# A third output-gate tile, one reset pattern for both scans, and a ScalarE table asked for by name, in a hybrid attention and recurrence block

## The chip, the cores and the metric

The kernel runs on one core of a Trainium2 chip. The metric is device microseconds for one execution; the time of a kernel is the median over its runs. Engines are named as in the profile: PE (TensorE matmul), PEld (its weight load), DVE (VectorE), ACT (ScalarE), POOL (GpSimd), SP (the queue that issues most transfers).

## The reference, cut to what matters

One encoder layer over 1024 tokens of width 1024. A shared RMSNorm and input projection feed a dilated windowed attention and a bidirectional gated recurrence; each branch is gated and projected, then the two are merged, projected and added to the input. The change is in the recurrence (8 heads of 128 channels, a forward scan and a backward scan):

```python
def gla_chunk_scan(q, k, v, log_f):
    b = jnp.cumsum(gc, axis=3)                 # of log_f, within a chunk
    q_t = qc * jnp.exp(b)
    k_t = kc * jnp.exp(-b)
    k_s = kc * jnp.exp(b_last[:, :, :, None, :] - b)
    a = jnp.where(lower, jnp.einsum('nbhik,nbhjk->nbhij', q_t, k_t), 0.0)
    o_intra = jnp.einsum('nbhij,nbhjv->nbhiv', a, vc)
    ...                                        # state = dec * state + k_s^T v;  o_inter = q_t state

def hgrn2_scan(q, i, z_f, lb):
    f = lb + (1.0 - lb) * jax.nn.sigmoid(z_f)
    return gla_chunk_scan(q, 1.0 - f, i, jnp.log(f))

o_fwd = hgrn2_scan(q_b, i_b, zf_fwd, lb_f)
o_bwd = ...                                    # the same on flipped inputs, with its own zf and lb
o_b = rms_norm(o_fwd + o_bwd, hg_norm_w[layer]) * jax.nn.silu(g_b)
```

So a head needs Sigmoid (forget gates, and the output gate of SiLU), Ln (of f, and inside the norm's inverse root), and Exp (of the sums, of the decays, and inside the norm's inverse root). [...]

## The kernel before, in words

The program is one long list of instructions for each engine, laid out by a planner in the source. `Plan` keeps a planned time for each engine and for each tile; every instruction goes through `Plan.note`, which adds an assumed duration and remembers which table ScalarE is assumed to hold (`table`: "sig", "exp" or "ln"; a switch is charged 1.28 us of planned ACT time). Work that isn't on the main line of projections is put down as tasks (`b.task`, for ACT, DVE, POOL or SP) or as products (`b.product`, for PE), each with the tiles that it needs; after every few projection matmuls the planner emits those whose inputs it takes to be ready. Each engine then runs its list in order, and waits at semaphores where data isn't there. So a changed planned duration or a free tile changes the order of everything behind it, on all engines.

The recurrence takes the span from about 950 to 1300 us. Per head h:

- four projections of 512 columns (`run_unit`, tiles gp) give the forget gates' inputs, evacuated by ACT into sk. Their fp32 operands are split into high and low parts; the weights' parts (whi, wlo) are made on ACT, with the rest added by a DMA of POOL.
- `logs(h)`: four Sigmoids over sk, `gates(h - 1)`, then four Ln into qr. Ahead of the Ln it asks by name for the table set that has both Ln and Exp. `gates` emits the Sigmoid of the output gate (gs from gb) of the previous head at once if its tile is there by the plan, or else leaves it as a task of its own.
- `sums`: a scan on DVE (Bc) that sums qr within chunks of 128, reset by a pattern of ones with a zero at each chunk's start (rst), then differences.
- `exps_b`: four Exp (km, km, qr, q); `decay_exp`: Exp of the decays G.
- `k_transpose` (PE, tile kT, from sk = km x G), a copy by ACT into an SBUF tile kT, `states` (PE, tile U, then the states S on DVE), `cross` (PE tiles X and Y, DVE into xa), `outputs` (PE tile oB, ACT squares it into on).
- `norm_out`, `norm_guess`, `scale_out`: DVE sums the squares (ssb); ACT does Ln, Exp and Square on 128x4 (oy, oz); DVE mends the factor; ACT scales oB into on. `out_transpose` (PE tile onT) then multiplies by the gate gb on DVE and stores.

The output gates' inputs lie in DRAM (gbD) and are loaded by SP into a ring of two tiles, gb, whose buffer comes free at `out_transpose`. Where a function's table isn't in, a load (ACT_TABLE_LOAD) stands in front of the instruction; where no set is asked for by name, the one for an Exp does not have Ln, and the one for an Ln does not have Exp.

Of the kernel before, what the change touches and what calls it, by code (L numbers as in the profile page):

```python
# [11 lines left out]
BF = mybir.dt.bfloat16  # L12
AF = mybir.ActivationFunctionType
OP = mybir.AluOpType
# [569 lines left out]
def hybrid_block(ctx, tc, a, out):  # L584
    b = Builder(ctx, tc, a)
    a_, v_, g_, t_, s_ = b.p.act, b.p.dve, b.p.pool, b.p.pe, b.p.sp
# [312 lines left out]
    for d in range(8):  # L899
        wh, wl = b.w[d]  # L900
        for j in range(4):
            c = slice(128 * j, 128 * j + 128)
# [666 lines left out]
    hp = bctx.enter_context(tc.tile_pool(name="hgrn", bufs=1))  # L1569
# [18 lines left out]
    a_.dma_start(mX, a["c_mx"])  # L1588
    a_.dma_start(mY, a["c_my"])
    BF = mybir.dt.bfloat16  # L1590
    rst = [hp.tile([128, 512], BF, name=f"rst{d}") for d in range(2)]
    for d in range(2):
        g_.memset(rst[d], 1.0)
        e = 0 if d == 0 else 127
        g_.memset(rst[d].rearrange("p (c t) -> p c t", c=4)[:, :, e:e + 1], 0.0)
    YB = hp.tile([128, 4, 64], F32, name="YB")
    g_.memset(YB, 0.0)

    ig_ring = b.ring(hp, "ig", 8, [128, 256])
    gb_ring = b.ring(hp, "gb", 2, [128, 512])  # L1600
    sk_ring = b.ring(hp, "sk", 7, [128, 512])
    qq_ring = b.ring(hp, "q", 2, [128, 512])
    qr_ring = b.ring(hp, "qr", 8, [128, 512])
# [50 lines left out]
    def c4(t):  # L1654
        return t.rearrange("p (c t) -> p c t", c=4)

    def start_head(h):
        st = dict(used={}, mm=[None, None], G=[None, None], QR={}, Q2={}, KM={}, S={}, s=0, qm=0, km=0)
        H[h] = st
        for d in range(2):  # L1660
            st["mm"][d] = mm_ring.get()
        b.task("act", [SK[h, d, u] for d, u in ORDER], lambda: logs(h), 4, lambda: qr_ring.soon(4))
# [6 lines left out]
    def gates(h):  # L1669
        for u in range(2):  # L1670
            here = lambda u=u: (h, u) in GB and b.when_all([GB[h, u]])
            if here():
                gate(h, u)
            else:
                b.task("act", [], lambda u=u: gate(h, u), 4, here)

    def logs(h):
        for d, u in ORDER:
            a_.activation(SK[h, d, u], SK[h, d, u], AF.Sigmoid)
        if h:  # L1680
            gates(h - 1)
        a_.preload_act_table_set("natural_log_exp_and_others")
        for d, u in ORDER:
            lf = qr_ring.get()
            a_.activation(lf, SK[h, d, u], AF.Ln, scale=omlb[:, d, h:h + 1], bias=lb[:, d, h:h + 1])
            b.task("dve", [lf], lambda d=d, u=u, lf=lf: sums(h, d, u, lf), 4, q2_ring.soon)

    def sums(h, d, u, lf):
        st = H[h]
        Bc = hp.tile([128, 512], F32, tag="Bc", name=b.name("Bc"), bufs=2)  # L1690
        if d == 0:
            v_.tensor_tensor_scan(Bc, rst[0], lf, 0.0, op0=OP.mult, op1=OP.add)
        else:
            v_.tensor_tensor_scan(Bc[:, ::-1], rst[1][:, ::-1], lf[:, ::-1], 0.0, op0=OP.mult, op1=OP.add)
        B4 = c4(Bc)
        at = slice(4 * u, 4 * u + 4)
        g_.tensor_copy(st["mm"][d][:, 0:2, at].rearrange("p k c -> p c k"), B4[:, :, 31 + d:97:64])
        g_.tensor_copy(st["mm"][d][:, 2, at], B4[:, :, LAST[d]])
        sec = slice(64, 128) if d == 0 else slice(0, 64)
        D1 = lf  # L1700
        v_.tensor_tensor(c4(D1), B4, B4[:, :, MID1[d]:MID1[d] + 1].to_broadcast([128, 4, 128]), op=OP.subtract)
        Q2 = q2_ring.get()
        v_.tensor_tensor(Q2, B4[:, :, sec], B4[:, :, MID2[d]:MID2[d] + 1].to_broadcast([128, 4, 64]),
                         op=OP.subtract)
        st["Q2"][d, u] = Q2
        b.task("act", [D1, Q2], lambda: exps_b(h, d, u, D1, Q2), 4, km_ring.soon)

    def exps_b(h, d, u, D1, Q2):
        st = H[h]
        fst, sec = (slice(0, 64), slice(64, 128)) if d == 0 else (slice(64, 128), slice(0, 64))  # L1710
        KM = km_ring.get()
        a_.activation(c4(KM)[:, :, fst], c4(D1)[:, :, fst], AF.Exp, scale=-1.0, bias=lomlb[:, d, h:h + 1])
        a_.activation(c4(KM)[:, :, sec], Q2, AF.Exp, scale=-1.0, bias=lomlb[:, d, h:h + 1])
        QR = D1
        a_.activation(QR, D1, AF.Exp)
        a_.activation(Q2, Q2, AF.Exp)
        st["QR"][d, u], st["KM"][d, u] = QR, KM
        b.task("dve", [KM], lambda: k_mul(h, d, u), 3)
        b.task("dve", [], lambda: q_mul(h, d, u), 5, lambda: (h, u) in QQ and b.when_all([QQ[h, u], QR, Q2]))
        if h == 7 and len(st["QR"]) == 4:  # L1720
            gates(h)
        if all((d, v) in st["QR"] for v in range(2)):
            b.task("dve", [st["mm"][d]], lambda: decay(h, d), 3, G_ring.soon)

    def decay(h, d):
        st = H[h]
        G = G_ring.get()
        mm = st["mm"][d]
        t = hp.tile([128, 8], F32, tag="Gt", name=b.name("Gt"), bufs=2)
        cur, nxt = (slice(0, 7), slice(1, 8)) if d == 0 else (slice(1, 8), slice(0, 7))  # L1730
        v_.tensor_tensor(t[:, cur], mm[:, 2, cur], mm[:, d, nxt], op=OP.add)
        v_.tensor_tensor(G[:, cur, d], t[:, cur], mm[:, d, cur], op=OP.subtract)
        v_.tensor_tensor(G[:, cur, 1 - d], t[:, cur], mm[:, 1 - d, cur], op=OP.subtract)
        b.task("act", [G], lambda: decay_exp(h, d, G, cur), 3)
        mm_ring.done(mm)

    def decay_exp(h, d, G, cur):
        a_.activation(G[:, cur, :], G[:, cur, :], AF.Exp)
        H[h]["G"][d] = G

    def k_mul(h, d, u):
        st = H[h]
        KM = st["KM"][d, u]
        v_.scalar_tensor_tensor(KM, SK[h, d, u], -1.0, KM, op0=OP.add, op1=OP.mult)
        st["km"] += 1
        b.task("dve", [KM], lambda: k_state(h, d, u), 3,
               lambda: st["G"][d] is not None and (h // 2, 4 * u + 3) in IG and b.when_all([st["G"][d]]))
        xready(h)
# [8 lines left out]
    def q_mul(h, d, u):  # L1757
        st = H[h]
        sec = slice(64, 128) if d == 0 else slice(0, 64)
        q = QQ[h, u]  # L1760
        v_.tensor_tensor(st["Q2"][d, u], st["Q2"][d, u], c4(q)[:, :, sec], op=OP.mult)
        v_.tensor_tensor(st["QR"][d, u], st["QR"][d, u], q, op=OP.mult)
        st["qm"] += 1
        if st["qm"] == 4:
            for v in range(2):
                qq_ring.done(QQ.pop((h, v)))
        xready(h)
# [125 lines left out]
    def norm_out(h, u, ps, on):  # L1893
        ss = tiny.tile([128, 4], F32, tag="ssb", name=b.name("ssb"), bufs=3)
        v_.tensor_reduce(ss, c4(on), axis=mybir.AxisListType.X, op=OP.add)
        b.task("act", [ss], lambda: norm_guess(h, u, ps, on, ss), 2)

    def norm_guess(h, u, ps, on, ss):
        y, y2 = (tiny.tile([128, 4], F32, tag=k, name=b.name(k), bufs=3) for k in ("oy", "oz"))
        a_.activation(y, ss, AF.Ln, scale=1.0 / 128, bias=eps)  # L1900
        a_.activation(y, y, AF.Exp, scale=-0.5)
        a_.activation(y2, y, AF.Square)

        def newton():
            v_.scalar_tensor_tensor(y2, ss, 128 * EPS, y2, op0=OP.add, op1=OP.mult)
            v_.scalar_tensor_tensor(y, y2, -384.0, y, op0=OP.add, op1=OP.mult)
            b.task("act", [y], lambda: scale_out(h, u, ps, on, y), 2)
        b.task("dve", [y2], newton, 2)

    def scale_out(h, u, ps, on, r):  # L1910
        for c in range(4):
            f0 = 128 * c
            a_.activation(on[:, f0:f0 + 128], ps[:, f0:f0 + 128], AF.Copy, scale=r[:, c:c + 1])
        b.bank.done(ps)
        b.product(7, [on], lambda: out_transpose(h, u, on),
                  lambda: stage.soon() and (h, u) in GI and b.when_all([GB[h, u]]), merge=False)
# [453 lines left out]
def _build(arrays):  # L2370
    import concourse.bacc as _bacc
    nc = _bacc.Bacc("TRN2", target_bir_lowering=False, num_devices=1)
    args = {n: nc.dram_tensor(f"in_{n}_dram", v.shape, mybir.dt.from_np(v.dtype), kind="ExternalInput").ap()
            for n, v in arrays.items()}
    out = nc.dram_tensor("out_0_dram", (S, D), F32, kind="ExternalOutput").ap()
    with tile.TileContext(nc) as tc:
        hybrid_block(tc, args, out)
    return nc
# [9 lines left out]
```

## Time and profile before

| what | value |
| --- | --- |
| median of 3 runs | 1510.41 us (1509.92 to 1513.04) |
| the profiled execution | 1511.62 us, its span 1509.8 us |
| PE busy, 950 to 1300 us | 329.21 of 350 us |
| ACT busy, 950 to 1300 us | 296.62 of 350 us |
| ACT_TABLE_LOAD in the whole program | 62, 79.5 us, 1283 ns each |
| of these between 950 and 1300 us | 58 |
| granted clock of PE, whole span | 0.994 |

A row of the timeline reads: start (us from the span's start), duration (us), engine, operation, out<-in, count, and in brackets the idle time of that engine just before and what ended it. A row of waits reads: engine and what it was about to write, what it waited for, us in total, times, the longest. A row of groups ends with the count, the busy time and the mean ns of one, and the idle time ahead of them. All instructions are recorded under one line of a helper (L57), so that the tiles' names tell them apart.

### The profile page before, as it was taken

The numbers are of one execution on the slowest core, as the hardware profiler recorded it, in microseconds if no ns is written. First come the engines' busy times: TensorE is split into PE (matmuls) and PEld (weight loads), VectorE is DVE, ScalarE is ACT, GpSimd is POOL, SyncE is SP. The second block draws the span as 40 slices with busy tenths as digits, with TensorE's granted clock in tenths as the row PEclk, the third lists the DMA queues.
The fourth block names the chain that finished last, engine by engine and source line by source line (L and its number), as shares of the span: only waits on it lengthen the run. The fifth ranks groups of instructions, "written<-read, shape, count | busy, mean of one in ns | idle before, by whom it ended". The sixth has DMA issues, their size and how long they took to land.

```text
span 1509.8 us, 23030 instructions
## 1 busy us (share of the span) xinstructions
PE 1473.4 (98%) x7965; PEld 1206.7 (80%) x7965; DVE 974.0 (65%) x1890; ACT 935.3 (62%) x1918; POOL 369.3 (24%) x376
## 2 busy tenths in 40 slices
PE   9999999999999999999999999999999899999998
PEld 7788888888888888877887777887788778787887
DVE  7791675778585888145443347487778767359973
ACT  5542665656575767256776432779889886647451
POOL 0032345354433333301102224321222211000011
PEclk9999999999999999999999999999999999999999
DMA  5455567576533243474643657633343342665464
GB/s 201 134 197 163 169 198 168 173 168 143 140 94 125 64 124 100 155 262 166 221 145 112 177 164 233 159 81 106 98 126 98 102 137 78 197 235 168 155 166 133
DMA packets 193577, 227.75 MB, mean 151 GB/s; under 512 B 45563, under 2 KB 118291, under 8 KB 192948
## 3 DMA queue, kind: packets, MB, share of 16 engines
q1 hardware_dynamic: 174084, 204.06, 41.4%
q0 software_dynamic: 11952, 21.76, 9.3%
q10 hardware_dynamic: 7424, 0.45, 0.3%
q8 instruction: 63, 1.03, 0.3%
q14 instruction: 54, 0.44, 0.1%
HBM read 166.08 MB, written 81.63 MB: 164 GB/s over the span
## 4 chain that ended last, share of the span: by engine, by line
PE 77%; ACT 11%; DVE 7%; issue 2%; DMA 2%; POOL 1%; SPq 0%; ACTq 0%; DVEq 0%; POOLq 0%
PE gp L57 27%; PE qA L57 15%; PE qE L57 7%; PE sA L57 6%; PE sE L57 4%; PE qC L57 4%; ACT L57 3%; PE o L57 3%; PE sc L57 2%; PE pT L57 2%; PE oB L57 2%; PE u L57 1%; PE nss L57 1%; ACT sk L57 1%; DVE ny L57 1%
## 5 line engine op out<-in xcount | busy, mean ns | idle before, releaser
L57 POOL TENSOR_TENSOR wlo<-qraw,whi 128x512 fp32r<-128x512 f32 x120 | 174.6, 1465 | 300.1 <-ACT whi L57 254.0
L57 ACT ACTIVATE whi<-qraw 128x512 fp32r<-128x512 f32 x168 | 104.5, 627 | 91.8 <-DVE qraw L57 39.3
L57 PE MATMUL gp<-hh,whi 128*128 128x512 f32 x336 | 139.8, 416 | 0.7 <-ACT stage L57 0.7
L57 PE MATMUL gp<-hh,wlo 128*128 128x512 f32 x336 | 132.8, 395 | 0.0
L57 PE MATMUL gp<-hl,whi 128*128 128x512 f32 x336 | 132.5, 394 | 0.0
L57 POOL TENSOR_TENSOR wlo<-raw,whi 128x512 fp32r<-128x512 f32 x48 | 66.1, 1385 | 240.4 <-ACT whi L57 227.5
L57 DVE CUSTOM_DVE_ANT_0 as<-sc,abias 128x192 f32<-128x192 f32 (+2 forms) x192 | 56.1, 348 | 101.4 <-PE sc L57 86.9
L57 DVE TENSOR_TENSOR qraw<-qraw,qraw 128x512 f32<-128x512 f32 x96 | 85.0, 886 | 34.9 <-POOL wlo L57 24.7
L57 PE MATMUL gp<-whi,hh 128*128 128x512 f32 x248 | 101.4, 409 | 2.1 <-ACT hh L57 1.4
L57 PE MATMUL gp<-whi,hl 128*128 128x512 f32 x248 | 98.0, 395 | 1.3 <-DVE hl L57 1.3
L57 PE MATMUL gp<-wlo,hh 128*128 128x512 f32 x248 | 97.3, 392 | 0.0
L57 ACT ACTIVATE whi<-raw 128x512 fp32r<-128x512 f32 x104 | 64.9, 625 | 47.3 <-PE gp L57 30.3
L57 ACT ACTIVATE as<-as,neg 128x192 f32<-128x192 f32 (+2 forms) x192 | 83.5, 440 | 8.3 <-DVE neg L57 8.3
L57 ACT ACTIVATE stage<-gp 128x512 f32<-128x512 f32 x60 | 35.6, 595 | 84.8 <-PE gp L57 64.2
L57 ACT ACT_TABLE_LOAD x62 | 79.5, 1283 | 4.8 <-DMA gb<-gbD 2.5
L57 PEld LDWEIGHTS gp<-hh,whi 128*128 128x128 f32 x336 | 64.0, 190 | 15.1 <-ACT stage L57 1.8
L57 PEld LDWEIGHTS gp<-hh,wlo 128*128 128x128 f32 x336 | 63.8, 190 | 14.4
L57 PE MATMUL qA<-hh,whi 128*128 128x512 f32 x192 | 75.1, 391 | 0.0
L57 PE MATMUL qA<-hh,wlo 128*128 128x512 f32 x192 | 75.0, 391 | 0.0
L57 PE MATMUL qA<-hl,whi 128*128 128x512 f32 x192 | 74.7, 389 | 0.0
L57 PEld LDWEIGHTS gp<-hl,whi 128*128 128x128 f32 x336 | 63.9, 190 | 10.6
L57 DVE SCALAR_TENSOR_TENSOR ny<-ny,spare 128x512 f32<-128x512 f32 x48 | 70.8, 1475 | 1.6
(299 smaller groups left out, 4134.5 us busy)
## 6 DMA issues: line engine op xcount, KB each, us to landing
raw<-in_w_in_dram SPq DMA_DIRECT2D x96, 256.0 KB, 2.6
qraw<-in_w_in_dram SPq DMA_DIRECT2D x96, 256.0 KB, 4.5
qkD<-ny SPq DMA_DIRECT2D x48, 256.0 KB, 2.8
sg<-sgD SPq DMA_DIRECT2D x32, 256.0 KB, 2.5
eraw<-wsD SPq DMA_DIRECT2D x32, 256.0 KB, 2.8
wlo<-in_w_in_dram POOLq DMA_DIRECT2D x31, 256.0 KB, 4.2
sgD<-stage SPq DMA_DIRECT2D x26, 256.0 KB, 2.0
ak<-qkD SPq DMA_DIRECT2D x6, 1024.0 KB
```

Of the source, the lines that this page charges most:

```text
L57: got = f(*args, **kw)
```

## The change

There are three edits. The ring gb has three tiles for two. The two reset patterns become one: the backward scan, which walks its data from the end, now reads the forward pattern from its start. And a helper `ln_exp` asks for the table set with Ln and Exp by name, if the planner doesn't already take a table with Ln to be in; it stands ahead of the Ln in `logs`, the Exp in `exps_b` and `decay_exp`, and the Ln in `norm_guess`.

```diff
-    rst = [hp.tile([128, 512], BF, name=f"rst{d}") for d in range(2)]
-    for d in range(2):
-        g_.memset(rst[d], 1.0)
-        e = 0 if d == 0 else 127
-        g_.memset(rst[d].rearrange("p (c t) -> p c t", c=4)[:, :, e:e + 1], 0.0)
+    rst = hp.tile([128, 512], BF, name="rst")
+    g_.memset(rst, 1.0)
+    g_.memset(rst.rearrange("p (c t) -> p c t", c=4)[:, :, 0:1], 0.0)
...
-    gb_ring = b.ring(hp, "gb", 2, [128, 512])
+    gb_ring = b.ring(hp, "gb", 3, [128, 512])
...
     def logs(h):
...
-        a_.preload_act_table_set("natural_log_exp_and_others")
+        ln_exp()
...
     def sums(h, d, u, lf):
...
-            v_.tensor_tensor_scan(Bc, rst[0], lf, 0.0, op0=OP.mult, op1=OP.add)
+            v_.tensor_tensor_scan(Bc, rst, lf, 0.0, op0=OP.mult, op1=OP.add)
         else:
-            v_.tensor_tensor_scan(Bc[:, ::-1], rst[1][:, ::-1], lf[:, ::-1], 0.0, op0=OP.mult, op1=OP.add)
+            v_.tensor_tensor_scan(Bc[:, ::-1], rst, lf[:, ::-1], 0.0, op0=OP.mult, op1=OP.add)
...
+    def ln_exp():
+        if b.p.table != "ln":
+            a_.preload_act_table_set("natural_log_exp_and_others")
+
     def exps_b(h, d, u, D1, Q2):
+        ln_exp()
...
     def decay_exp(h, d, G, cur):
+        ln_exp()
...
     def norm_guess(h, u, ps, on, ss):
...
+        ln_exp()
         a_.activation(y, ss, AF.Ln, scale=1.0 / 128, bias=eps)
         a_.activation(y, y, AF.Exp, scale=-0.5)
```

The order of instructions shows it at two engines. First ACT at the norms of head 2 (on is the squared output, sk the evacuated gate input of a later head, oy and oz the norm's factors). Before:

```order
L57 ACTIVATE on_10564<-oB_10552 128x512
L57 ACTIVATE sk_10572<-gp_10497 128x512
L57 ACT_TABLE_LOAD
L57 ACTIVATE oy_10576<-ssb_10574,eps 128x4
L57 ACT_TABLE_LOAD
L57 ACTIVATE oy_10576<-oy_10576 128x4
L57 ACTIVATE oz_10577<-oy_10576 128x4
L57 ACTIVATE on_10597<-oB_10585 128x512
L57 ACTIVATE on_10564<-oB_10552,oy_10576 128x128 x4
```

After:

```order
L57 ACTIVATE on_10510<-oB_10498 128x512
L57 ACTIVATE sk_10518<-gp_10459 128x512
L57 ACTIVATE whi_10520<-raw_10095 128x512
L57 ACTIVATE wlo_10521<-whi_10520 128x512
L57 ACTIVATE oy_10526<-ssb_10524,eps 128x4
L57 ACTIVATE oy_10526<-oy_10526 128x4
L57 ACTIVATE oz_10527<-oy_10526 128x4
L57 ACTIVATE G_10493<-G_10493 128x14
L57 ACTIVATE on_10558<-oB_10546 128x512
```

The two loads around the norm's Ln are gone, and a weight split and a decay's Exp stand between the steps of the norm.

Then PE, at the transposes that follow these norms (kT turns the next head's keys, onT the normed output, U makes the state updates). Before:

```order
L57 MATMUL gp_10599<-hh_104,wlo_9787 128x512
L57 MATMUL U_10719<-ig_10171,kT_10661 128x128
L57 MATMUL U_10719<-ig_10173,kT_10661 128x128
L57 MATMUL U_10719<-ig_10175,kT_10661 128x128
L57 MATMUL onT_10726<-ident,on_10564 128x128 x4
L57 MATMUL onT_10733<-ident,on_10597 128x128 x4
L57 MATMUL X_10740<-qr_10277,km_10418 64x128
```

After:

```order
L57 MATMUL gp_10560<-hl_101,whi_9785 128x512
L57 MATMUL gp_10560<-hh_100,wlo_9786 128x512
L57 MATMUL kT_10632<-ident,sk_9962 128x128 x4
L57 MATMUL kT_10639<-ident,sk_10055 128x128 x3
L57 MATMUL onT_10645<-ident,on_10510 128x128 x4
L57 MATMUL gp_10652<-hbh,whi_9611 128x512
```

Before, both onT come after the head's two groups of U; after, the first follows the transposes of the keys, which stand back to back, ahead of any U.

Last ACT at the gates of head 4 (gs), which come with the Sigmoid (sk) and the Ln (qr) of head 5. Before:

```order
L57 ACTIVATE sk_11066<-sk_11066 128x512
L57 ACTIVATE gs_11157<-gb_11084 128x512
L57 ACT_TABLE_LOAD
L57 ACTIVATE qr_11160<-sk_10851,lbv,omlb 128x512
L57 ACTIVATE qr_11162<-sk_10974,lbv,omlb 128x512
L57 ACTIVATE qr_11164<-sk_11145,lbv,omlb 128x512
L57 ACTIVATE qr_11166<-sk_11066,lbv,omlb 128x512
L57 ACTIVATE kT_11173<-kT_11168 128x512
L57 ACT_TABLE_LOAD
L57 ACTIVATE gs_11239<-gb_11224 128x512
```

After:

```order
L57 ACTIVATE sk_11171<-sk_11171 128x512
L57 ACTIVATE sk_11073<-sk_11073 128x512
L57 ACTIVATE gs_11183<-gb_10709 128x512
L57 ACTIVATE gs_11185<-gb_11107 128x512
L57 ACT_TABLE_LOAD
L57 ACTIVATE qr_11188<-sk_10872,lbv,omlb 128x512
L57 ACTIVATE qr_11190<-sk_10983,lbv,omlb 128x512
```

Both gates stand ahead of the Ln under one pair of loads; before, one of the two came after the Ln, between two loads of its own.

## The prediction

> **What bounds the kernel now.** I read the page's busy shares first, then the busy time by stretch, then the waits of PE in the stretch that stands out, then ACT's instructions in order of time just ahead of those waits.
>
> ```profile
> PE 1473.4 (98%) x7965; PEld 1206.7 (80%) x7965; DVE 974.0 (65%) x1890; ACT 935.3 (62%) x1918; POOL 369.3 (24%) x376
> ...
> 950.00:1000.00 50.00, 50.00 (x292) 41.97 (x291) 30.02 (x62) 44.60 (x81) 14.20 (x22) 1.00 0.56 135
> 1000.00:1300.00 300.00, 279.21 (x1876) 236.63 (x1876) 215.63 (x470) 252.02 (x481) 59.45 (x97) 0.98 0.40 105
> ```
>
> The first line is the page's; the others give a stretch's length, the busy time of PE, PEld, DVE, ACT and POOL (with instructions), the granted clock, the DMA share and GB/s. PE is busy for 1473.4 of 1509.8 us, so only 36.4 us of the span can be won by closing its waits. The recurrence (950 to 1300 us) holds 20.8 us of that (300 - 279.21), with a granted clock of 0.98 on top. So the whole effect of this change, which touches the recurrence alone, lies within those 20.8 us, what the low clock costs, and whatever it adds. ACT is busy for 84% of that stretch (252.02 of 300), DVE for 72%.
>
> ```profile
> PE U L57 <- ACT kT L57: 6.7, 4, 3.7
> PE kT L57 <- DVE sk L57: 5.9, 3, 2.7
> PE oB L57 <- DVE S L57: 4.5, 5, 1.4
> PE onT L57 <- ACT on L57: 2.2, 2, 1.2
> PE Y L57 <- DVE xa L57: 1.0, 1, 1.0
> PE oB L57 <- DVE xa L57: 0.4, 1, 0.4
> ```
>
> This is the whole list of PE's waits between 950 and 1300 us (total us, times, longest). Three kinds end on ACT directly or on DVE work queued behind ACT. What ACT does meanwhile:
>
> ```profile
> L57 ACT ACT_TABLE_LOAD x58 | 74.4, 1283 | 3.5 <-DMA gb<-gbD 2.5
> ...
> 1087.64 1.28 ACT L57 ACT_TABLE_LOAD   x1
> 1090.96 1.28 ACT L57 ACT_TABLE_LOAD   x1
> 1092.25 0.30 ACT L57 ACTIVATE oy<-ssb,eps 128x4 f32<-128x4 f32 x1
> 1092.57 1.28 ACT L57 ACT_TABLE_LOAD   x1
> 1093.87 0.20 ACT L57 ACTIVATE oy<-oy 128x4 f32<-128x4 f32 x1
> 1095.84 0.57 ACT L57 ACTIVATE kT<-kT 128x512 f32<-128x512 f32 x1
> 1096.47 2.08 PE L57 MATMUL U<-ig,kT 128*128 128x128 f32 x8 [3.68 <-ACT kT L57]
> ```
>
> 58 of the program's loads of ScalarE's table fall into this stretch: 74.4 us of ACT, at 1283 ns each, the next instruction starting 10 to 20 ns after the load's end. Of head 2's two norms, each small Ln and each small Exp has a load of its own in front. In that time PE runs out of other work, its transposed keys lie in PSUM uncopied, and U starts 3.68 us late. The other large waits have the same pairs ahead of them:
>
> ```profile
> 1174.46 1.28 ACT L57 ACT_TABLE_LOAD   x1
> 1176.23 0.17 DVE L57 SCALAR_TENSOR_TENSOR oz<-ssb,oz 128x4 f32<-128x4 f32 x1 [3.71 <-ACT oz L57]
> 1176.51 2.22 DVE L57 TENSOR_TENSOR sk<-km,G 128x512 f32<-128x512 f32 x4
> 1177.34 1.09 PE L57 MATMUL kT<-ident,sk 128*128 128x128 f32 x4 [2.73 <-DVE sk L57]
> 1220.30 0.63 PE L57 MATMUL kT<-ident,sk 128*128 128x128 f32 x4 [2.73 <-DVE sk L57]
> 1293.94 1.11 PE L57 MATMUL onT<-ident,on 128*128 128x128 f32 x4 [1.15 <-ACT on L57]
> ...
> 1050.63 1.28 ACT L57 ACT_TABLE_LOAD   x1
> 1057.42 0.82 PE L57 MATMUL U<-ig,kT 128*128 128x128 f32 x5 [1.63 <-ACT kT L57]
> 1130.74 1.28 ACT L57 ACT_TABLE_LOAD   x1
> 1137.97 1.16 PE L57 MATMUL U<-ig,kT 128*128 128x128 f32 x8 [0.69 <-ACT kT L57]
> ```
>
> At 1176 us DVE, in order, stands 3.71 us at the norm's oz with the keys' product (sk) queued behind it, and PE stands at the transpose of sk. The trace also holds a head without these loads: head 0, whose gates both came ahead of its successor's Ln, so that the table with Ln and Exp stayed in.
>
> ```profile
> 1006.13 0.30 ACT L57 ACTIVATE oy<-ssb,eps 128x4 f32<-128x4 f32 x1 [1.28 <-DVE ssb L57]
> 1006.46 0.20 ACT L57 ACTIVATE oy<-oy 128x4 f32<-128x4 f32 x1
> 988.00:1020.00 32.00, 31.59 (x237) 27.26 (x236) 26.80 (x60) 23.81 (x55) 7.34 (x13) 1.00 0.27 64
> 1005.44 0.49 PE L57 MATMUL oB<-ig,xa 128*128 128x128 f32 x2 [0.41 <-DVE xa L57]
> ```
>
> Ln and Exp follow each other directly, and in 32 us PE stands for 0.41 us in all. That is the nearest row to what the change makes of the other heads.
>
> **The change, part by part.** The named table and the third tile go together: the order of the changed kernel has 33 loads of the table for 62, so 29 go, of which 27 are norms' loads (28 down to 1), 2 fewer stand ahead of km and 1 fewer ahead of gs, and 1 is new ahead of G. 29 x 1.283 = 37.2 us of ACT's 252. What of it lies beside PE's other work is worth nothing; what counts is the waits above.
>
> - U behind kT, 6.7 us: three of the four waits (3.68, 1.63, 0.69 us) have a norm's pair of loads 4 to 9 us ahead, and ACT works without a pause from there; the fourth (0.70) follows the two loads of a gate that now joins the other ahead of Ln. All 6.7 go.
> - kT behind sk, 5.9 us in three waits: twice 2.73 us and a short one, each behind a norm's pair. All go.
> - onT behind on, 2.2 us: both follow a norm's pair. All go.
> - oB behind S, Y and oB behind xa, 5.9 us: DVE's own chain. I let them stand. Below: they go too, as 0.41 us in head 0's 32 us suggests (5.9 us more gained). Above: in three heads (1, 4 and 5) the last product ahead of oB (X, Y or U) now has six projection matmuls behind it, where it had 12 to 18, so each could wait as long as the longest such wait:
>
> ```profile
> 1279.15 0.49 PE L57 MATMUL oB<-S,qr 128*128 128x128 f32 x2 [1.39 <-DVE S L57]
> 1197.40 1.16 PE L57 MATMUL U<-ig,kT 128*128 128x128 f32 x8 [0.70 <-ACT kT L57]
> ```
>
>   That is 3 x 1.39 = 4.2 us lost. Head 0 is the like case (X, Y, six projection matmuls, oB), so I take its 0.41 each, 1.2 us, and one wait of 0.70 us (the row of U just shown) where a copy of kT now stands behind two weight splits: 1.9 us lost.
> - The clock. After the three longest waits PE ran at a halved clock for a while:
>
> ```profile
> 1096.40:1103.00 6.60, 6.53 (x28) 5.94 (x28) 5.04 (x13) 4.49 (x13) 1.40 (x2) 0.56 0.59 159
> 1177.50:1184.00 6.50, 6.50 (x58) 5.62 (x57) 5.49 (x13) 4.51 (x9) 2.26 (x3) 0.75 0.81 218
> 1220.50:1228.00 7.50, 7.50 (x61) 6.63 (x60) 6.46 (x15) 6.59 (x13) 2.26 (x3) 0.77 0.82 219
> ...
> 1060.00:1070.00 10.00, 10.00 (x75) 8.33 (x74) 6.41 (x12) 9.93 (x16) 2.69 (x6) 1.00 0.67 179
> ```
>
>   Lost full-speed time: 0.44 x 6.60 + 0.25 x 6.50 + 0.23 x 7.50 = 2.9 + 1.6 + 1.7 = 6.2 us, inside PE's busy time. No wait is left above 1.4 us, and behind the 1.63 us wait the clock stayed at 1.00 (last row), so all 6.2 go. The ends are 0, if new waits of that length turn up, and 6.2. [...]
> - The shared reset pattern: POOL loses two MEMSETs in front of the recurrence, and the backward scans read the pattern forwards. The 32 scans, forward and backward together, keep within 16 ns of each other, so the direction in which they read their operands does not show:
>
> ```profile
> L57 DVE TENSOR_TENSOR_SCAN Bc<-rst,qr x32: 1211/1220/1227, 966.4 to 1249.7; 128x512 f32<-128x512 bf16 x32
> L57 POOL MEMSET rst<- x4: 116/321/525, 946.1 to 947.3; 128x512 bf16 x2, 128x4 bf16 x2
> ```
>
>   Nothing, both: POOL is busy for 14 of 50 us there, and PE does not stand at all between 950 and 1000 us. The ends for the 16 backward scans are 16 x 16 ns = 0.3 us of DVE, either way.
> - The gates:
>
> ```profile
> L57 ACT ACTIVATE gs<-gb x16: 614/630/635, 986.7 to 1271.8; 128x512 f32<-128x512 f32 x16
> ```
>
>   Seven more gate Sigmoids (10 for 3) now stand ahead of the Ln of the next head, 0.63 us each on ACT, beside the projections' matmuls. SP issues the loads of gb up to one head earlier. Behind the Sigmoid on ACT wait the four Ln, DVE's scans behind these, and at last PE. The one wait of ACT for such a load was 2.5 us (row of the loads above). Taken at nothing, since the moved Sigmoid is mostly that of the tile loaded a head earlier; if that cover is gone, see the last rival.
>
> Sum: 6.7 + 5.9 + 2.2 + 6.2 - 1.9 = 19.1 us. The profiled execution took 1511.62 us, 1.2 us above the median of 1510.41; from the median the time is 1491.3, say 1491 us.
>
> **The rivals.** (a) DVE takes ACT's place. It is busy for 72% of the stretch and would hold the same work in 20 us less, 77%; its product and state chains already end waits of 5.9 us. For: the order is packed closer at oB. Against: head 0, with DVE at 26.80 of 32 us (84%), kept PE busy. If half of the 14.8 us of waits returns under DVE's name, with one dip of the clock (1.7 us), the gain is 19.1 - 7.4 - 1.7 = 10 us: 1500 us. (b) The waits only move: an order fixed ahead puts PE at other places and loses as much there. For: PE, DVE and SP are all reordered from head 1 on, so no old place is simply kept. Against: 37.2 us of ACT are gone for good. 1507 to 1513 us. (c) Slower: the gate ahead of Ln. If each of the seven moved Sigmoids waits for gb as the one did (2.5 us), the four Ln come late, DVE's first scan with them, and PE stands with a dip of 1.7 us each: 7 x 4.2 = 29.4 us lost against 19.1 gained, 1521 us. It decides from 19.1 / 7 = 2.7 us per moved gate. Against: one such wait in 16 loads, and a load now mostly precedes its use by a head.
>
> **How the numbers follow.** The forecast (1483 to 1496 us) has 0.62: its low end takes the 5.9 us of DVE's waits and the 1.9 us of new ones out as well (1483.5), its high end has 4.2 + 0.7 instead of 1.9 us lost, and a dip. Rival (a), 1496 to 1507, has 0.23; (b) 0.08; (c) 0.07. The runs of before spread over 3.1 us, so 0.2% (3.0 us) is about what can be told from no change: faster 0.85, same 0.08, slower 0.07. The range is 1483 to 1505: it leaves out (b), (c) and the end of (a).
>
> **What would show it.** Right: 29 loads in the stretch instead of 58; Ln, Exp and Square of a norm within 0.8 us of each other; PE's waits for kT copies, sk and on near zero and 4 to 8 us of waits on S and xa left; the clock at 1.00 from 1000 to 1300 us; the same work of the end stage simply earlier. Half right: waits of PE on S, xa or sk of 1 to 3 us with no load ahead. Wrong: ACT standing at gs for gb, or PE's idle time in the recurrence still near 20 us.

## The result, and the profile after

The changed kernel takes 1485.36 us (median of 4 runs, 1483.24 to 1486.29) where the kernel before takes 1511.72 us: the ratio is 0.9824, 95% interval 0.9805 to 0.9842. A second series gave 1482.60 us against 1510.78, ratio 0.9817 (0.9800 to 0.9834). So it is faster by 26 to 28 us; the forecast was 19.1 us less, 1491 us, range 1483 to 1505. The first series lies 2.4 us inside the range's low end, the second 0.4 us below it.

The page's busy shares after, the two stretches of the recurrence, and the loads of ScalarE's table between 950 and 1300 us:

```profile
PE 1463.4 (99%) x7965; PEld 1201.1 (81%) x7965; DVE 976.3 (66%) x1890; ACT 897.6 (61%) x1889; POOL 369.2 (25%) x374
...
950.00:1000.00 50.00, 49.48 (x288) 41.14 (x287) 31.06 (x67) 45.39 (x83) 14.18 (x22) 1.00 0.62 147
1000.00:1300.00 300.00, 297.15 (x1991) 252.36 (x1990) 227.30 (x487) 229.44 (x476) 59.73 (x97) 1.00 0.49 127
...
L57 ACT ACT_TABLE_LOAD x30 | 38.5, 1283 | 2.4 <-DMA gb<-gbD 1.9
```

In the 300 us from 1000 us on, PE now stands still for 2.9 us where it stood for 20.8, and its clock stays at 1.00. (The stretch now holds some 28 us of the next stage, too.) ACT lost 37.7 us of busy time over the program. The waits of PE between 950 and 1300 us, the whole list:

```profile
PE oB L57 <- DVE S L57: 0.8, 1, 0.8
PE gp L57 <- issue: 0.7, 1, 0.7
PE gp L57 <- ACT sk L57: 0.5, 1, 0.5
PE U L57 <- ACT kT L57: 0.4, 2, 0.2
PE oB L57 <- DVE xa L57: 0.4, 1, 0.4
PE kT L57 <- DVE sk L57: 0.3, 1, 0.3
```

The wait on "issue" is not new: it opens the next stage, and the kernel before has it at 1301.26 us, just behind this window.

The norm of head 2 on ACT, in order of time: Ln, Exp and Square follow each other within 0.76 us, and no load is between them.

```profile
1077.68 0.28 ACT L57 ACTIVATE oy<-ssb,eps 128x4 f32<-128x4 f32 x1
1077.99 0.21 ACT L57 ACTIVATE oy<-oy 128x4 f32<-128x4 f32 x1
1078.23 0.21 ACT L57 ACTIVATE oz<-oy 128x4 f32<-128x4 f32 x1
```

### The profile page after: what moved, and what is told of

Read it like the earlier page. It is cut to its first block, busy times and chain, and to the rows that moved or that the text cites. A ratio compares the mean times of both kernels' runs of the same rounds, so it can differ in the third digit from the quotient of the medians.

```text
span 1481.5 us, 23010 instructions
## 1 busy us (share of the span) xinstructions
PE 1463.4 (99%) x7965; PEld 1201.1 (81%) x7965; DVE 976.3 (66%) x1890; ACT 897.6 (61%) x1889; POOL 369.2 (25%) x374
## 5 line engine op out<-in xcount | busy, mean ns | idle before, releaser
L57 DVE SCALAR_TENSOR_TENSOR ny<-ny,spare 128x512 f32<-128x512 f32 x48 | 76.0, 1584 | 1.6
L57 ACT ACTIVATE ny<-ny 128x512 f32<-128x512 f32 x96 | 60.8, 633 | 6.5 <-DVE ny L57 3.4
```

The costliest lines, as they stand in the source:

```text
L57: got = f(*args, **kw)
```

## The experiments

Gains below are against the kernel before on the same chip: 1511.73 us for the first four, 1510.78 us for the others.

**The loads gone, the order kept.** The planner isn't told of the names, so that it lays out what it laid out before. Only ACT's list is shorter by 27 loads. (The lines that keep `held` up to date, and the calls, are left out here.)

```diff
...
+    def ln_exp():
+        if b.p.held != "ln":                 # the table that is really in, followed in Plan.note
+            a_.real.preload_act_table_set("natural_log_exp_and_others")
+            b.p.held = "ln"
...
```

> The table is asked for by name at the same places, but the planner is not told, so that every engine keeps the order of before, word for word, and only 27 loads are gone from ACT's list. Theory A: the waits of PE on kT copies, sk and on close (14 us) and the clock stays up (6 us), so 1492 us or less. On the waits on S and xa (5.9 us before): if they are DVE's own chain, as predicted, they stay at 5 to 6 us; if they were ACT's lateness handed on, they fall below 2 us and the time is 1485 to 1488 us. Theory B: the order is what matters, so 1500 us or more.

Measured: 1487.38 us, ratio 0.9834 (0.9818 to 0.9850), a gain of 24.4 us. Of its waits of PE between 950 and 1300 us those that bear on this, and its stretch from 1000 us:

```profile
PE oB L57 <- DVE S L57: 4.1, 5, 1.4
PE gp L57 <- ACT xh L57: 1.2, 1, 1.2
PE Y L57 <- DVE xa L57: 1.0, 1, 1.0
...
PE U L57 <- ACT kT L57: 0.7, 1, 0.7
PE oB L57 <- DVE xa L57: 0.4, 1, 0.4
...
1000.00:1300.00 300.00, 291.56 (x1965) 248.40 (x1965) 224.28 (x483) 230.23 (x472) 59.43 (x97) 1.00 0.47 124
```

So the loads alone carry most of the gain, in an order that is the old one word for word: the waits on the norms' pairs are gone (U keeps the 0.7 us that followed a gate's loads, which are still there), and the clock stays at 1.00. The waits on S and xa stay, 5.5 us for 5.9: they are not ACT's lateness handed on, but belong to the order. The time alone could not have told, since 1487.38 us lies in the range that was set for lateness handed on (1485 to 1488 us), too; the waits decide. (The wait on xh lies in the next stage, which starts at 1276 us here.)

**The order kept, the loads back.** The mirror: the changed kernel's order on every engine, but outside of `logs` the request for the table is told to the planner only and not emitted, so that 52 loads stand for 33.

```diff
...
-        ln_exp()
+        ln_exp(True)
...
-    def ln_exp():
+    def ln_exp(real=False):
         if b.p.table != "ln":
-            a_.preload_act_table_set("natural_log_exp_and_others")
+            if real:
+                a_.preload_act_table_set("natural_log_exp_and_others")
+            else:
+                b.p.note("act", "preload_act_table_set", ("natural_log_exp_and_others",), {})
...
```

> The order of the changed kernel on every engine, word for word, but the planner's requests for the table are not emitted outside of logs, so that the loads come back where Ln and Exp meet: 52 for 33. Theory A: 19/29 of the gain is lost, 1500 to 1506 us, with halved clock again behind waits of 2.7 us or more. Theory B: the order holds the gain, 1490 us or less.

Measured: 1504.81 us, ratio 0.9950 (0.9933 to 0.9967): 6.9 us of gain are left, and the 19 loads cost 19.5 us against the changed kernel. Its longest waits of PE:

```profile
PE onT L57 <- ACT on L57: 5.4, 5, 2.4
PE U L57 <- ACT kT L57: 4.9, 4, 3.0
PE kT L57 <- DVE sk L57: 2.7, 1, 2.7
PE oB L57 <- DVE S L57: 0.8, 1, 0.8
```

The three kinds of wait on the norms are back, in the new order; the wait on S is as short as in the changed kernel. In the waits the two halves come apart: the loads make those on kT, sk and on, the order those on S and xa. In the times they do not add up so neatly, since the 6.9 us that are left stand for the order and for nine loads that this order saves by itself.

**The named table alone**, with two gb tiles and two patterns, as the changed kernel otherwise (against which the edit is shown):

```diff
-    rst = hp.tile([128, 512], BF, name="rst")
...
+    rst = [hp.tile([128, 512], BF, name=f"rst{d}") for d in range(2)]
...
-    gb_ring = b.ring(hp, "gb", 3, [128, 512])
+    gb_ring = b.ring(hp, "gb", 2, [128, 512])
...
```

> The named table alone: two gb tiles and two reset patterns as before, 35 loads for 62, a new order. Theory A (the norms' loads made PE wait): 27 of the 29 loads are gone, so nearly the whole gain, 1486 to 1491 us. Theory B (the gates ahead of Ln, which the third tile allows, and the order that goes with them, carry the gain): at most a third of it, 1503 us or more.

Measured: 1489.61 us, ratio 0.9851 (0.9832 to 0.9870), 22.1 us. The waits on the norms are gone here too. What remains is above all one wait, of 1.0 us in each of six heads:

```profile
PE Y L57 <- DVE xa L57: 5.8, 6, 1.0
...
PE oB L57 <- DVE xa L57: 0.4, 1, 0.4
PE oB L57 <- DVE S L57: 0.3, 2, 0.2
```

**The third tile and the shared pattern alone**, without `ln_exp`: 57 loads.

> The third gb tile and the shared pattern alone: 57 loads for 62, a new order. Theory A: 5 of 29 loads, so about 5/29 of 26 us, 1505 to 1509 us, with waits of PE behind norms' pairs of loads still there. Theory B: most of the gain, 1495 us or less.

Measured: 1508.25 us, ratio 0.9976 (0.9966 to 0.9986), 3.5 us. The longest waits stand behind norms' pairs as before:

```profile
PE kT L57 <- DVE sk L57: 6.8, 3, 2.7
PE onT L57 <- ACT on L57: 4.4, 4, 2.4
PE U L57 <- ACT kT L57: 3.4, 3, 2.9
```

The gains rise with the loads that go: 58 loads stand between 950 and 1300 us before; 53 give 3.5 us, 49 give 6.9, 32 give 22.1 and 24.4, 30 give 26.4 and 28.2. That is 0.7 to 1.0 us for a load that goes, of the 1.3 us that it takes on ACT. Only two pairs have the same order on both sides: 24.4 us for the 26 loads that go from the kernel before, 19.5 us for the 19 that come back to the changed one, 0.9 and 1.0 us for a load. In the others the order changes with the loads.

**The shared pattern alone**, in the kernel before:

```diff
...
+    rst = hp.tile([128, 512], BF, name="rst")
...
+            v_.tensor_tensor_scan(Bc[:, ::-1], rst, lf[:, ::-1], 0.0, op0=OP.mult, op1=OP.add)
...
```

> The shared reset pattern alone, in the kernel before: the same order on PE and ACT, 62 loads, two MEMSETs fewer on POOL. As predicted it is worth nothing: 1508 to 1515 us, the scans at 1.22 us. The rival, that the backward scans gain or lose by the direction in which they read the pattern, gives a mean of the scans off by more than 16 ns and a changed time.

Measured: 1510.18 us, ratio 0.9995 (0.9985 to 1.0006). The scans keep their time, a median of 1218 ns for 1220:

```profile
L57 DVE TENSOR_TENSOR_SCAN Bc<-rst,qr x32: 1211/1218/1226, 965.3 to 1246.6; 128x512 f32<-128x512 bf16 x32
```

What is left for it is space: a tile of gb takes 2 KB of each partition, and the pattern that goes gives 1 KB back. Whether the third tile would fit without it was not tried.

**Needless loads elsewhere**: the changed kernel with two more loads ahead of each of 16 evacuations before the recurrence.

```diff
     def evac_qe(h, u):
...
+            for table in ("exp_and_others", "natural_log_exp_and_others"):
+                a_.real.preload_act_table_set(table)
```

> The changed kernel with two needless loads of ScalarE's table ahead of each of 16 evacuations before the recurrence, where ACT is busy for a fifth to a third of the time: 55 groups of loads, about 38 loads (49 us of ACT) more, untold to the planner, so that PE keeps its order. If a load costs only where PE waits behind ACT, 1485 to 1489 us (the evacuation of each projection comes 2.6 us later into a ring of three PSUM tiles). If a load costs in itself, by ACT's time or by what it fetches, 1500 us or more.

Measured: 1497.84 us, ratio 0.9920 (0.9901 to 0.9938); the changed kernel on the same chip took 1482.60 us, so 38 more loads (49 us of ACT) cost 15.2 us. Both expectations missed. The stretch from 850 to 900 us and the waits of PE between 800 and 950 us:

```profile
850.00:900.00 50.00, 44.13 (x177) 34.33 (x178) 11.26 (x23) 31.77 (x41) 8.69 (x7) 0.94 0.47 122
...
PE al L57 <- DVE og L57: 2.5, 1, 2.5
PE al L57 <- ACT alB L57: 2.4, 3, 1.5
PE gp L57 <- ACT stage L57: 2.0, 2, 1.0
```

A share of busy time misled me: the merge of the attention groups has its chain through ACT there (alB), though in the changed kernel ACT is busy for only 16.97 of these 50 us. Part of the cost is the clock, 0.94 in the row above (3.0 us) and 0.97 in the 50 us from 950 us (1.5 us), where the changed kernel has 1.00. Two thirds of the loads' time stayed hidden, one third did not. So this run does not show that a load off PE's path is free.

**The gates behind the Ln**: the changed kernel, with every gate of heads 0 to 6 left as a task of its own behind the Ln of the next head (39 loads).

```diff
-            if here():
+            if h == 7 and here():
```

> The changed kernel, with every gate Sigmoid of heads 0 to 6 left as a task behind the Ln of the next head (39 loads for 33, three gb tiles, a new order). If the gates ahead of Ln close the waits on S and xa (1.2 us in the changed kernel, 6.5 us with the named table alone), these come back to 4 us or more and the time is 1488 to 1493 us. If the third tile itself or the mere re-planning closes them, they stay below 2 us and the time is 1485 to 1487 us.

Measured: 1486.37 us, ratio 0.9845 (0.9827 to 0.9863), 3.8 us above the changed kernel's median, with intervals that overlap. The waits:

```profile
PE oB L57 <- DVE S L57: 2.1, 3, 1.3
PE Y L57 <- ACT kT L57: 1.4, 3, 0.9
PE U L57 <- ACT kT L57: 0.9, 3, 0.4
PE oB L57 <- DVE xa L57: 0.8, 1, 0.8
```

2.9 us on S and xa lie between the two expectations (4 or more, below 2); the time lies in the range of the second (1485 to 1487 us). How much of what the order gave is owed to the gates' place and how much to the tile is not settled.

**The changed kernel again**, for the comparison on one chip:

> The changed kernel once more, on the chip of the three others: 1483 to 1487 us.

Measured: 1482.60 us, the median of 5 runs from 1481.63 to 1486.23, 0.4 us below what was expected.

## Why the prediction was right, and where it was off

- U behind kT, kT behind sk, onT behind on (14.8 us predicted to go): they went from 14.8 to 0.7 us. Right, and shown to be the loads' doing from both sides: without the loads they go in the old order, with the loads they return in the new one.
- The clock (6.2 us): 1.00 from 950 to 1300 us. Right.
- "DVE's own chain. I let them stand", with 1.9 us of new waits on top: this is the term that was mis-sized. The waits on S, Y and xa went from 5.9 to 1.2 us, and the only new one is 0.5 us on sk. The cause was named rightly, since without the loads the old order keeps 5.5 us of them; what I did not see is that the new order closes them. I had priced six projections behind the last product as a loss in heads 1, 4 and 5; in none of the three does oB wait now. At head 3 it can be read. With the old order (the loads gone), the rows of DVE and PE that matter, in order of time:

```profile
1101.28 1.22 DVE L57 TENSOR_TENSOR_SCAN Bc<-rst,qr 128x512 f32<-128x512 bf16 x1
...
1102.63 1.72 PE L57 MATMUL U<-ig,kT 128*128 128x128 f32 x14
...
1104.11 0.75 DVE L57 COPY_PREDICATED xa<-mX,X 128x512 f32<-128x512 int32 x1 [0.54 <-POOL xa L57]
...
1106.42 2.33 DVE L57 SCALAR_TENSOR_TENSOR S<-S,G,U 128x128 f32<-128x128 f32 x6
...
1108.81 0.49 PE L57 MATMUL oB<-S,qr 128*128 128x128 f32 x2 [1.44 <-DVE S L57]
```

  The scans, xa and six state updates stand in one row on DVE, and oB waits for the last of them. In the changed kernel at the same head:

```profile
1098.57 0.85 DVE L57 TENSOR_TENSOR xa<-xa,YB 64x256 f32<-64x256 f32 x2
...
1102.82 1.23 DVE L57 TENSOR_TENSOR_SCAN Bc<-rst,qr 128x512 f32<-128x512 bf16 x1
...
1105.63 1.10 DVE L57 SCALAR_TENSOR_TENSOR S<-S,G,U 128x128 f32<-128x128 f32 x3
...
1106.79 0.49 PE L57 MATMUL oB<-S,qr 128*128 128x128 f32 x2
```

  xa comes ahead of the scans, only three updates are left behind them, and oB does not wait. Between U and oB stand twelve projection matmuls in both orders, so these make no difference. I counted them, and priced fewer as a loss; what decides here is what stands ahead of S on DVE. Heads 4 and 5 bear it out: in the old order xa and a scan stand on DVE ahead of the last three updates, and oB waits 0.50 and 1.00 us (the loads gone); in the changed kernel xa comes behind these updates, and oB does not wait.
- The sum counted a wait from the end that the profile shows for the matmul before it, and that end is modelled. Before the wait of 3.68 us, in the kernel before:

```profile
1092.15 0.40 PE L57 MATMUL gp<-hl,whi 128*128 128x512 f32 x1
1092.39 0.40 PE L57 MATMUL gp<-hh,wlo 128*128 128x512 f32 x1
```

  A matmul shows 0.40 us, but the next starts 0.24 us after it, so that each wait behind such a matmul costs 0.16 us more than its idle time. With some 10 fewer waits that is 1.6 us, an estimate, since not every wait has such a matmul ahead of it. With it, the account of the profiles is 18.3 (waits, 20.7 to 2.4, the one on "issue" left out) + 6.2 + 1.6 = 26.1 us, against 28.3 us between the two spans (1509.8 and 1481.5) and 26.4 us between the medians. The 2.2 us that are missing between the spans stay open.
- The gates: ACT waited for gb once, 1.9 us, although ten gates stand ahead of Ln. Rival (c), which needed 2.7 us at each of seven, did not come about. Rival (a) did not either: DVE's busy share rose (227.30 us of 300 for 215.63), and PE's waits on S, Y and xa fell. Nor did rival (b): the waits went and did not turn up elsewhere.
- So the mechanism held, and the gain was forecast low by over a quarter (19.1 us of 26.4). The misses nearly all have one sign (waits on S and xa, new waits, overlap); none made up for another.

## What to carry to other kernels

Count a table load, or any fixed cost of an engine, by what the bound engine waits for behind it, and look for a stretch of the same trace where the cost is absent: head 0 had no loads between Ln and Exp, and PE stood there for 0.41 us in 32. Where a planner lays out the order, test the cost with the order held fixed and the order with the cost held fixed; here the first gave 24.4 of the 26 to 28 us, and the second 2 to 4 us (the changed kernel against the loads gone, 30 loads for 32). A wait that is not the change's target can still go when the order is laid out anew, so it belongs in the range at its full size, and it is read from what stands ahead of the producer on its engine, not only from the filler ahead of the consumer.

## What the runs showed of the hardware

Whether PE's clock is halved after a wait does not follow from the wait's length alone. Below are the stretches of about 6.6 us behind waits of 2.9 us (U behind kT), 2.4 us (onT behind on) and twice up to 2.7 us (kT behind sk) in the kernel with the third tile alone, and behind waits of 3.0, 2.4 and 2.7 us (the same three kinds) in the one with the loads back. The figure right behind POOL's busy time is the granted clock; one halved stretch of 3.4 us brings it to about 0.75 here.

```profile
1053.20:1060.00 6.80, 6.80 (x54) 6.16 (x56) 6.52 (x16) 4.15 (x8) 1.94 (x3) 0.75 0.62 154
1093.40:1100.00 6.60, 6.58 (x29) 5.34 (x29) 6.56 (x14) 2.97 (x8) 1.67 (x3) 0.74 0.35 109
1212.30:1219.00 6.70, 6.70 (x62) 5.76 (x63) 6.59 (x15) 6.16 (x14) 2.27 (x3) 1.00 0.78 199
1253.00:1260.00 7.00, 7.00 (x68) 6.16 (x69) 6.86 (x16) 3.76 (x10) 2.80 (x4) 1.00 0.83 189
```

```profile
1053.90:1060.50 6.60, 6.60 (x65) 5.92 (x66) 6.32 (x16) 5.52 (x10) 2.26 (x3) 1.00 0.71 166
1092.50:1099.00 6.50, 6.47 (x29) 5.24 (x29) 6.46 (x14) 2.98 (x8) 1.47 (x3) 0.74 0.29 104
1132.50:1139.00 6.50, 6.46 (x29) 5.26 (x30) 6.18 (x15) 3.10 (x10) 0.00 (x0) 0.74 0.33 107
```

Behind the waits of 2.4 us it was halved in both kernels, and behind the one of 2.9 us too; behind the one of 3.0 us it was not, and of the three of kT behind sk it was halved behind one. These rows do not show what tells them apart.

Where a halved stretch begins can be read in the kernel before, behind its waits of 3.68, 2.73 and 2.73 us (stretches cut where the clock changes):

```profile
1095.36:1102.19 6.83, 5.72 (x21) 5.15 (x22) 5.51 (x13) 4.77 (x13) 1.40 (x2) 0.50 0.56 150
1177.28:1180.69 3.41, 3.35 (x10) 2.79 (x11) 3.41 (x8) 1.72 (x6) 1.40 (x2) 0.50 0.69 139
1221.65:1225.06 3.41, 3.41 (x15) 3.04 (x14) 2.57 (x6) 2.51 (x5) 0.67 (x2) 0.50 0.74 162
```

Between these stretches, and from 1000 us to the first and from the last to 1300 us, the clock is 1.00. They do not begin where the waits end (1096.47, 1177.34 and 1220.30 us), but 1.11 and 0.06 us earlier and 1.35 us later. Their starts lie 81.92 and 44.37 us apart, 24 and 13 steps of 3.413 us. An estimate from these rows is that the clock changes at such steps, and that what counts is how much of a wait lies in the step ahead of the halved stretch: here 2.57, 2.67 and 2.06 us. The wait of 1.63 us, which ends at 1057.42 us, would lie whole in one step, and behind it the clock stayed at 1.00. Why the first halved stretch lasts two steps (6.83 us) stays open. Whether the same tells the seven waits above apart is not shown, and no run was made to test it.

So a gap of 2.4 us and more, here, is to be priced with the 1.7 us of a dip (3.41 us at half speed) as a possible, not a sure, addition.
